# Attention scores of two heads from matmuls over the two halves of the array's rows

## The chip, the cores and the metric

The kernel runs on one core of one Trainium2 chip. The metric is the device time of one execution in microseconds (us). A core has TensorE (PE in the profile, its weight loads PEld), which multiplies a stationary operand, loaded beforehand, with a moving one and writes into PSUM; VectorE (DVE), ScalarE (ACT) and GpSimd (POOL), which work on SBUF and, the first two, on PSUM; and SyncE (SP), which issues the DMAs.

## The reference

Two decoder layers on a sequence of 512 tokens of width 1024, in float32. Layer 0 runs two groups of heads side by side, layer 1 one group of 16 heads; each is followed by a projection, a layer norm and a squared-ReLU MLP. What matters here are the scores, each a product of a query and a key of 64 numbers per head:

```python
# layer 0, A: 4 heads x 2 maps
s = jnp.einsum('bqhcd,bshcd->bhcqs', qb, kr)
p = jax.nn.softmax(jnp.where(mask, s, -jnp.inf), axis=-1)
pd = p[:, :, 0] - lam * p[:, :, 1]
...
# layer 0, B: 8 query heads on 2 k/v groups; compressed, selected and window branch
sc = jnp.einsum('bqghd,bngd->bghqn', qb, kc)
ss = jnp.where(valid_s, jnp.einsum('bqghd,bgqkld->bghqkl', qb, kg), -jnp.inf)
sw = jnp.einsum('bqghd,bsgd->bghqs', qb, kwb)
...
# layer 1, C: 16 heads with a cumulative forget bias
s = jnp.einsum('bqhd,bshd->bhqs', qb, kf) + cq[..., None] - c[:, :, None, :]
p = jax.nn.softmax(jnp.where(mask, s, -jnp.inf), axis=-1)
return jnp.einsum('bhqs,bshd->bqhd', p, vf)
```

With these sizes the selected branch covers all earlier tokens and the window all of the sequence, so both are causal softmaxes over 512 keys. That makes 8 + 16 + 16 = 40 causal softmaxes of one head each: 8 in A, 16 in B (8 heads, 2 branches), 16 in C.

## The kernel before

TensorE takes operands in fp32r, a float32 form of less precision. To keep float32 accuracy the kernel splits each operand into a high part (rounded to fp32r) and a low part (the rest) and adds three products: high x high, high x low, low x high. A head has only 64 rows of q and k, so the high and low part of one head are stacked on the 128 partitions. `stacks_q` (line 233) makes one tile with q's high part on one half and its low part on the other; `stacks_k` (line 250) makes two tiles, `ka` with k's high and low part and `kb` with the same two exchanged. In `softmax` (line 262) two matmuls over 128 rows, lines 270 and 271, then give all four products of a head (the low x low one comes for free). `split2` (line 243) makes each high and low part for one head of 64 partitions; lines 257 and 258 copy k's parts into the exchanged tile.

`softmax` goes over four tiles of 128 queries. Tile i has scores against (i+1) x 128 keys, so the moving operand is 128, 256, 384 and 512 columns wide. The scores fall into a PSUM bank of the tag "s", of which there are two. Line 274 (VectorE) adds the mask or the bias and takes a minimum, line 275 (ScalarE) makes the exponential and its sum. `scale_p` divides by the sums; `transpose_p` turns the probabilities by TensorE (line 288), through the tag "t", and splits them; `pv` (lines 303, 304) multiplies them with V.

Layer 0's attention runs the pieces of `EVEN_ORDER`: projections of q, k, v (`nat_chunk`, lines 180 to 182), compression, the branches, the heads of A (`diff_head`) and pairs of heads of B (`nsa_pair`). `nsa_pair` begins with the compressed branch: lines 810 and 811 multiply over 64 rows only. Layer 1's attention (`odd_attention`) goes over four groups of four heads; its projections of q and k are in `tr_block` (lines 193 to 195).

The order on each engine is not the order of the code: when the program is built, a scheduler places each instruction where it expects its inputs to be ready, so that TensorE's projections, transposes and products with V of one head stand between the scores of another. On the chip each engine takes its instructions in that built order.

Of the kernel before, what the change touches and what calls it, by code (L numbers as in the profile page):

```python
# [15 lines left out]
P = 128  # L16
SEQ = 512
NT = 4
# [13 lines left out]
QB = 6  # L32
KB = 6
# [27 lines left out]
def tile_trunk(ctx: ExitStack, tc: tile.TileContext, x, xt_in, ln_gain, ln_bias, w_up, w_down, w_ie, w_oe, lam_p, subln,  # L61
# [66 lines left out]
    lo_engine, rope_engine = [V], [V]  # L128

# [113 lines left out]
    def split2(src, hi, lo, scale):  # L243
        A.activation(hi, src, AF.Copy, scale=scale)
        if scale == 1.0:
            V.tensor_tensor(lo, src, hi.bitcast(F32), op=ALU.subtract)
        else:
            V.scalar_tensor_tensor(lo, src, scale, hi.bitcast(F32), op0=ALU.mult, op1=ALU.subtract)
# [12 lines left out]

    def softmax(ap, q, k, bias=None):

        p = new(ap, "p", [P, 1280], bufs=2)
        sm = new(ap, "sm", [P, 8], bufs=4)
        for i in range(NT):
            w = (i + 1) * P
            s = bank("s")
            qs = slice(i * P, (i + 1) * P)
            T.matmul(s[:, :w], q[:, qs], k[0][:, :w], start=True, stop=False)  # L270
            T.matmul(s[:, :w], q[:, qs], k[1][:, :w], start=False, stop=True)
            pv = p[:, OFF[i]:OFF[i] + w]
            add = mask[:, 512 - w:512] if bias is None else bias[:, OFF[i]:OFF[i] + w]
            V.tensor_tensor_reduce(pv, s[:, :w], add, 1.0, 3e38, ALU.add, ALU.min, sm[:, i:i + 1])  # L274
            A.activation(pv, pv, AF.Exp, bias=sm[:, i:i + 1], scale=-1.0, accum_out=sm[:, 4 + i:5 + i])  # L275
        return p, sm

# [857 lines left out]
```

## Time and profile before

| | us |
|---|---|
| median of 3 runs (lowest, highest) | 1274.55 (1274.54, 1275.23) |
| the profiled execution | 1273.6 |
| its span, first to last instruction | 1271.5 |
| TensorE busy | 1237.5 |
| VectorE busy | 878.2 |
| ScalarE busy | 647.3 |
| GpSimd busy | 301.2 |

The span is the time between the first and the last instruction that the profile shows; some 2 us of the execution lie around it. Busy time is the union of an engine's instructions. TensorE's matmuls are pipelined: the next one starts before the last one's end, so its durations add up to more than its busy time. The attention of layer 0 lies between about 60 and 300 us, that of layer 1 between about 680 and 890 us; the rest is projections and MLPs.

### The profile page before, as it was taken

What the parts mean: (1) busy time and instruction counts of PE and PEld (TensorE: products, weight loads), DVE (VectorE), ACT (ScalarE), POOL (GpSimd) and SP (SyncE); (2) the same over time, 40 slices, a digit from 0 to 9 for tenths busy, and PEclk for the clock granted to TensorE, in tenths of its full rate; (3) what the DMA queues carried; (4) which work ended last, traced back from release to release, by engine and by line L of the source; (5) the groups of instructions that cost most, each with busy time, mean ns of one, the idle gap of its engine ahead of it and who ended that gap; (6) DMA issues with size and microseconds to landing.
All of it is one profiled execution on the core that took longest, in us unless ns stands there. A gap on an engine that the chain in (4) does not pass through costs nothing.

```text
span 1271.5 us, 18398 instructions
## 1 busy us (share of the span) xinstructions
PE 1237.5 (97%) x7046; PEld 1079.2 (85%) x7046; DVE 878.2 (69%) x1602; ACT 647.3 (51%) x1185; POOL 301.2 (24%) x321
## 2 busy tenths in 40 slices
PE   7999998998999999999998999999999999999997
PEld 7999897898988888888887889889988888888886
DVE  5476768787859478495456788879767948669454
ACT  5266766764355454454423576767334445354530
POOL 1125565354200000000044354556510000000012
PEclk9999999999999999999999999999999999999999
DMA  7321121034414405234014322323630522505201
GB/s 274 114 87 54 34 67 35 5 129 138 167 61 132 133 25 175 67 96 146 17 50 150 101 84 92 92 88 129 231 112 23 182 84 68 164 34 159 73 17 50
DMA packets 46758, 125.15 MB, mean 98 GB/s; under 512 B 4672, under 2 KB 5184, under 8 KB 46672
## 3 DMA queue, kind: packets, MB, share of 16 engines
q1 hardware_dynamic: 46672, 123.99, 30.3%
q8 instruction: 55, 0.90, 0.3%
q14 instruction: 31, 0.25, 0.1%
HBM read 119.75 MB, written 4.23 MB: 98 GB/s over the span
## 4 chain that ended last, share of the span: by engine, by line
PE 86%; DVE 6%; DMA 3%; ACT 2%; issue 1%; POOL 1%; SPq 0%; DVEq 0%; ACTq 0%; POOLq 0%
PE g L193 11%; PE g L194 11%; PE g L195 11%; PE g L180 4%; PE g L181 4%; PE g L182 4%; PE s L478 3%; PE t L288 3%; PE s L479 3%; PE s L480 2%; DMA wraw<-w_up 2%; PE s L270 2%; PE o L480 2%; PE t L478 2%; PE o L478 2%; PE o L479 2%
## 5 line engine op out<-in xcount | busy, mean ns | idle before, releaser
L194 PE MATMUL g<-big,wlo 128*128 128x512 f32 x608 | 236.8, 391 | 0.0
L195 PE MATMUL g<-big,whi 128*128 128x512 f32 x608 | 236.6, 390 | 0.0
L193 PE MATMUL g<-big,whi 128*128 128x512 f32 x608 | 236.3, 390 | 0.0
L144 ACT ACTIVATE whi<-wraw 128x1024 fp32r<-128x1024 f32 (+3 forms) x120 | 125.3, 1045 | 112.5 <-DMA wraw<-w_up 37.1
L212 POOL TENSOR_TENSOR ve<-ve,nhalf 128x1 f32<-128x1 f32 x16 | 15.9, 991 | 647.0 <-DVE ve L211 647.0
L145 DVE TENSOR_TENSOR wlo<-wraw,whi 128x1024 fp32r<-128x1024 f32 (+2 forms) x69 | 84.3, 1228 | 96.5 <-ACT whi L144 96.4
L145 POOL TENSOR_TENSOR wlo<-wraw,whi 128x1024 fp32r<-128x1024 f32 (+2 forms) x51 | 123.4, 2425 | 94.6 <-ACT whi L144 82.3
L195 PEld LDWEIGHTS g<-big,whi 128*128 128x128 f32 x608 | 114.2, 188 | 23.6
L193 PEld LDWEIGHTS g<-big,whi 128*128 128x128 f32 x608 | 114.2, 188 | 23.2 <-issue 0.2
L194 PEld LDWEIGHTS g<-big,wlo 128*128 128x128 f32 x608 | 114.1, 188 | 23.1
L180 PE MATMUL g<-whi,big 128*128 128x256 f32 (+2 forms) x416 | 120.3, 289 | 0.6 <-DVE fz L946 0.4
L182 PE MATMUL g<-whi,big 128*128 128x256 f32 (+2 forms) x416 | 119.6, 287 | 0.0
L181 PE MATMUL g<-wlo,big 128*128 128x256 f32 (+2 forms) x416 | 119.1, 286 | 0.0
L414 DVE TENSOR_TENSOR wlo<-wdr,whi 128x1024 fp32r<-128x1024 f32 x72 | 87.4, 1218 | 44.4 <-ACT whi L413 44.4
L275 ACT ACTIVATE p<-p,sm 128x128 f32<-128x128 f32 (+3 forms) x160 | 89.2, 558 | 45.7 <-DVE sm L274 44.5
L395 ACT ACTIVATE big<-g 128x512 f32<-128x512 f32 x64 | 38.2, 597 | 134.4 <-PE g L195 134.4
L413 ACT ACTIVATE whi<-wdr 128x1024 fp32r<-128x1024 f32 x72 | 75.9, 1055 | 48.2 <-PE t L480 29.6
L321 POOL TENSOR_TENSOR p<-p,rs 128x128 f32<-128x128 f32 (+2 forms) x108 | 71.5, 688 | 93.2 <-DVE rs L970 40.4
L180 PEld LDWEIGHTS g<-whi,big 128*128 128x128 f32 x416 | 79.1, 190 | 2.2 <-ACT fv L114 0.6
L182 PEld LDWEIGHTS g<-whi,big 128*128 128x128 f32 x416 | 79.1, 190 | 0.7 <-issue 0.4
L181 PEld LDWEIGHTS g<-wlo,big 128*128 128x128 f32 x416 | 79.1, 190 | 0.6
L116 DVE TENSOR_TENSOR ptl<-t,pth 128x384 fp32r<-128x384 f32 (+1 forms) x108 | 63.1, 595 | 21.1 <-ACT pth L114 20.4
(313 smaller groups left out, 3093.0 us busy)
## 6 DMA issues: line engine op xcount, KB each, us to landing
wraw<-w_up SPq DMA_DIRECT2D x64, 512.0 KB, 3.7
wdr<-w_down SPq DMA_DIRECT2D x64, 512.0 KB, 4.7
wraw<-w_io SPq DMA_DIRECT2D x22, 512.0 KB, 3.3
wraw<-w_ie SPq DMA_DIRECT2D x18, 512.0 KB, 3.7
v<-w SPq DMA_DIRECT2D x8, 512.0 KB, 5.2
wraw<-w_oe SPq DMA_DIRECT2D x8, 512.0 KB, 3.6
cb<-c_dram SPq DMA_DIRECT2D x16, 256.0 KB, 3.2
wraw<-w_oo SPq DMA_DIRECT2D x8, 512.0 KB, 3.4
```

The source lines that it names most:

```text
L144: A.activation(hi[:, c], raw[:, c], AF.Copy)
L145: (eng or lo_engine[0]).tensor_tensor(lo[:, c], raw[:, c], hi[:, c].bitcast(F32), op=ALU.subtract)
L180: T.matmul(bv[:, tt], xh, h, start=first, stop=False)
L181: T.matmul(bv[:, tt], xh, l, start=False, stop=False)
L182: T.matmul(bv[:, tt], xl, h, start=False, stop=last)
L193: T.matmul(b[:, a:e], h[:, cs], xh, start=k == 0, stop=False)
L194: T.matmul(b[:, a:e], l[:, cs], xh, start=False, stop=False)
L195: T.matmul(b[:, a:e], h[:, cs], xl, start=False, stop=k == 7)
L275: A.activation(pv, pv, AF.Exp, bias=sm[:, i:i + 1], scale=-1.0, accum_out=sm[:, 4 + i:5 + i])
L413: A.activation(hi, r, AF.Copy)
L414: V.tensor_tensor(lo, r, hi.bitcast(F32), op=ALU.subtract)
L478: T.matmul(bv, hh, us[m][0][:, k], start=first, stop=False, skip_group_check=True)
```

## The change

The high and low parts are no longer stacked within a head. Two heads share a tile: the first head's 64 rows on partitions 0 to 63, the second's on 64 to 127, with one tile for the high parts and one for the low (`pair_q`, `pair_k`; `both_k` where two query heads share one key head, so that it stands on both halves). Each of the three products of a head is a matmul over 64 rows, the two heads' in turn, into a bank of each head. Per tile of queries the pair has six matmuls of 64 rows, where it had four of 128 rows. A token asks the scheduler to keep the six in this order; other matmuls may stand between them. `diff_head` takes its two maps as the pair, `nsa_pair` two query heads, `odd_attention` two heads. `pv` now makes the transposes of a group just ahead of its products, and p has three (layer 0) or four (layer 1) buffers for two. In the compressed branch one matmul of 64 columns serves two heads, three per pair and query tile.

```diff
+    bufs_ = dict(q=3, k=5, p=3)
...
-    def stacks_q(ap, b, scale):
-        r = []
-        for e in range(2):
-            q = new(ap, "q", [P, SEQ], F32R, bufs=QB)
-            own, oth = slice(64 * e, 64 * e + 64), slice(64 - 64 * e, 128 - 64 * e)
-            split2(b[own], q[own], q[oth], scale)
-            r.append(q)
-        return r
-    def stacks_k(ap, b, tag, bufs):
-        r = []
-        for e in range(2):
-            ka = new(ap, tag + "a", [P, SEQ], F32R, bufs=bufs)
-            kb = new(ap, tag + "b", [P, SEQ], F32R, bufs=bufs)
-            own, oth = slice(64 * e, 64 * e + 64), slice(64 - 64 * e, 128 - 64 * e)
-            split2(b[own], ka[own], ka[oth], 1.0)
-            A.activation(kb[oth], ka[own].bitcast(F32), AF.Copy)
-            V.tensor_copy(kb[own], ka[oth].bitcast(F32))
-            r.append((ka, kb))
-        return r
+    def pair_q(ap, b, scale):
+        q = [new(ap, f"q{c}", [P, SEQ], F32R, bufs=bufs_["q"]) for c in "hl"]
+        split(b, q[0], q[1], scale)
+        return q
+    def pair_k(ap, b):
+        k = [new(ap, f"k{c}", [P, SEQ], F32R, bufs=bufs_["k"]) for c in "hl"]
+        split(b, k[0], k[1])
+        return k
+    def both_k(ap, b, e):
+        k = [new(ap, f"k{c}", [P, SEQ], F32R, bufs=bufs_["k"]) for c in "hl"]
+        own = slice(64 * e, 64 * e + 64)
+        for r in (own, slice(64 - 64 * e, 128 - 64 * e)):
+            A.activation(k[0][r], b[own], AF.Copy)
+            V.tensor_tensor(k[1][r], b[own], k[0][own].bitcast(F32), op=ALU.subtract)
+        return k
+    def in_order(tok, ins):
+        tc.stamp_issue_order_token(ins.ins, tok)
     def softmax(ap, q, k, bias=None):
-        p = new(ap, "p", [P, 1280], bufs=2)
-        sm = new(ap, "sm", [P, 8], bufs=4)
+        p = [new(ap, "p", [P, 1280], bufs=bufs_["p"]) for _ in range(2)]
+        sm = [new(ap, "sm", [P, 8], bufs=4) for _ in range(2)]
         for i in range(NT):
             w = (i + 1) * P
-            s = bank("s")
+            s = [bank("s") for _ in range(2)]
             qs = slice(i * P, (i + 1) * P)
-            T.matmul(s[:, :w], q[:, qs], k[0][:, :w], start=True, stop=False)
-            T.matmul(s[:, :w], q[:, qs], k[1][:, :w], start=False, stop=True)
-            pv = p[:, OFF[i]:OFF[i] + w]
...
+            tok = nm("scores")
+            for n, (a, c) in enumerate(((0, 0), (1, 0), (0, 1))):
+                for e in range(2):
+                    rows = slice(64 * e, 64 * e + 64)
+                    in_order(tok, T.matmul(s[e][:, :w], q[a][rows, qs], k[c][rows, :w], start=n == 0, stop=n == 2))
+            for e in range(2):
+                pv = p[e][:, OFF[i]:OFF[i] + w]
+                add = mask[:, 512 - w:512] if bias is None else bias[e][:, OFF[i]:OFF[i] + w]
+                V.tensor_tensor_reduce(pv, s[e][:, :w], add, 1.0, 3e38, ALU.add, ALU.min, sm[e][:, i:i + 1])
+                A.activation(pv, pv, AF.Exp, bias=sm[e][:, i:i + 1], scale=-1.0, accum_out=sm[e][:, 4 + i:5 + i])
...
+    def pv(ap, o, p, v, start, stop):
         for grp in ((0,), (1,), (2, 3)):
...
+            pt = transpose_p(ap, p, grp)
             for j in grp:
...
         def nsa_cmp(g, qs):
             b = bank("s")
             for i in range(NT):
-                for h in range(4):
-                    o_ = b[:, i * 128 + h * 32:i * 128 + h * 32 + 32]
-                    for a in range(2):
-                        T.matmul(o_, qs[h][:, i * P:(i + 1) * P], kcs[:, a, g * 32:g * 32 + 32], start=a == 0, stop=a == 1)
+                for pr in range(2):
+                    o_ = b[:, i * 128 + pr * 64:i * 128 + pr * 64 + 64]
+                    for n, (a, c) in enumerate(((0, 0), (1, 0), (0, 1))):
+                        T.matmul(o_, qs[pr][a][:, i * P:(i + 1) * P], kcs[:, c, g].rearrange("p e n -> p (e n)"),
+                                 start=n == 0, stop=n == 2)
...
         def diff_head(kb, qk, v, h):
-            qs, kk = qk
-            p1, s1 = softmax(ap, qs[1], kk[1])
-            p0, s0 = softmax(ap, qs[0], kk[0])
+            (p0, p1), (s0, s1) = softmax(ap, *qk)
...
     def odd_attention(ap, mh, ml):
         wi = Weights(w_io)
+        bufs_.update(q=2, k=2, p=4)
...
-                    p, sm = softmax(ap, qs[e], kk[e], bias)
...
+                p, sm = softmax(ap, q, k, bias)
```

How the built order of TensorE moves, at two places. The first is the odd layer's first group, at the widest tile of a head. Before (`s` are score banks, `nka`, `nkb` the stacked tiles of k, `g` banks of a projection, `whi`, `wlo` its weights):

```order
L195 MATMUL g_1225_7224<-big_1106_6440,whi_1179_7042 128x512
L270 MATMUL s_1189_7067<-nka_1171_7022,q_1168_6991 128x384
L271 MATMUL s_1189_7067<-nkb_1172_7023,q_1168_6991 128x384
L270 MATMUL s_1190_7072<-nka_1171_7022,q_1168_6991 128x512
L271 MATMUL s_1190_7072<-nkb_1172_7023,q_1168_6991 128x512
L180 MATMUL g_1278_7421<-whi_1272_7410,big_1103_6437 128x256
```

And now, where `kh`, `kl` are the pair's high and low parts of k, `qh`, `ql` those of q, and the two numbers of `s` are the two heads' banks; score matmuls are line 269 now, and the lines of `nat_chunk` are 179 to 181:

```order
L179 MATMUL g_1323_7508<-whi_1319_7450,big_1145_6477 128x256
L269 MATMUL s_1236_7128<-kh_1211_7058,qh_1208_7029 128x512
L180 MATMUL g_1323_7508<-wlo_1320_7451,big_1145_6477 128x256
L181 MATMUL g_1323_7508<-whi_1319_7450,big_1146_6478 128x256
L179 MATMUL g_1323_7508<-whi_1319_7450,big_1145_6477 128x256
L180 MATMUL g_1323_7508<-wlo_1320_7451,big_1145_6477 128x256
L269 MATMUL s_1237_7129<-kh_1211_7058,qh_1208_7029 128x512
L269 MATMUL s_1236_7128<-kh_1211_7058,ql_1209_7030 128x512
L269 MATMUL s_1237_7129<-kh_1211_7058,ql_1209_7030 128x512
L269 MATMUL s_1236_7128<-kl_1212_7059,qh_1208_7029 128x512
L269 MATMUL s_1237_7129<-kl_1212_7059,qh_1208_7029 128x512
L181 MATMUL g_1323_7508<-whi_1319_7450,big_1146_6478 128x256
```

The head's scores stood together with the next tile's; now the first of the pair's six stands by itself, four projection matmuls follow, then the other five. The second place is the even layer, B's pair 01, the scores of the second branch. Before (`pth`, `ptl` are split transposes, `ident` belongs to a transpose):

```order
L288 MATMUL t_218_1440<-ident_2_69,p_211_1411 128x128 x2
L270 MATMUL s_232_1490<-nka_127_911,q_79_572 128x512
L271 MATMUL s_232_1490<-nkb_128_912,q_79_572 128x512
L304 MATMUL o_176_1278<-ptl_208_1394,v_109_753 128x256
L303 MATMUL o_176_1278<-pth_207_1393,v_109_753 128x128
L304 MATMUL o_176_1278<-ptl_208_1394,v_109_753 128x128
L288 MATMUL t_221_1449<-ident_2_69,p_211_1411 128x128 x3
```

And now, at the same scores (line 286 is a transpose now, lines 303 and 304 are still the products with V):

```order
L269 MATMUL s_223_1429<-kl_128_914,qh_78_573 128x384
L304 MATMUL o_175_1263<-ptl_205_1373,v_89_595 128x512
L286 MATMUL t_209_1388<-ident_2_69,p_177_1269 128x128 x3
L303 MATMUL o_175_1263<-pth_207_1382,v_89_595 128x384
L304 MATMUL o_175_1263<-ptl_208_1383,v_89_595 128x384
L269 MATMUL s_225_1440<-kh_127_913,qh_78_573 128x512
L303 MATMUL o_175_1263<-pth_210_1392,v_89_595 128x256
L269 MATMUL s_226_1441<-kh_127_913,qh_78_573 128x512
L269 MATMUL s_225_1440<-kh_127_913,ql_79_574 128x512
```

Score matmuls stood in twos among transposes and products with V; they stand in sixes, or as one and five, among the same. Over the whole program the matmuls over 64 rows (scores, and the two of the compressed branch) stand in 129 unbroken runs (68 in layer 0, 61 in layer 1; 45 of them a single matmul, 38 of five, 17 of six), where before only lines 810 and 811 are such, in 8 runs of two.

## Rows read from the trace of the kernel before

**Rows 1.** The page: busy time of each engine, and the chain of waits by engine.
```profile
PE 1237.5 (97%) x7046; PEld 1079.2 (85%) x7046; DVE 878.2 (69%) x1602; ACT 647.3 (51%) x1185; POOL 301.2 (24%) x321
...
PE 86%; DVE 6%; DMA 3%; ACT 2%; issue 1%; POOL 1%; SPq 0%; DVEq 0%; ACTq 0%; POOLq 0%
```

**Rows 2.** Two stretches: start:end, length, then busy us of each engine (instructions), clock, DMA.
```profile
128.00:256.00 128.00, 120.19 (x871) 108.91 (x871) 96.96 (x277) 92.22 (x243) 68.80 (x114) 0.99 0.12 40
700.00:890.00 190.00, 189.56 (x1179) 167.88 (x1178) 155.41 (x355) 127.13 (x278) 96.74 (x78) 0.99 0.30 98
```

**Rows 3.** Groups by line and shape: count | busy us, mean ns | idle before.
```profile
L270 PE MATMUL s<-nka,q 128*128 128x512 f32 x40 | 16.7, 418 | 0.0
...
L271 PE MATMUL s<-nkb,q 128*128 128x128 f32 x40 | 11.0, 275 | 0.0
...
L258 DVE CAST nkb<-nka 64x512 fp32r<-64x512 f32 x28 | 15.6, 556 | 0.9
...
L246 DVE TENSOR_TENSOR nka<-g,nka 64x512 fp32r<-64x512 f32 x22 | 15.2, 689 | 1.6 <-ACT nka L244 1.0
```

**Rows 4.** Timeline of TensorE, odd layer: start us, duration us, line, tiles, shapes.
```profile
715.03 0.34 PE L270 MATMUL s<-nka,q 128*128 128x384 f32 x1
715.20 0.34 PE L271 MATMUL s<-nkb,q 128*128 128x384 f32 x1
715.38 0.39 PE L270 MATMUL s<-nka,q 128*128 128x512 f32 x1
715.61 0.40 PE L271 MATMUL s<-nkb,q 128*128 128x512 f32 x1
715.84 0.28 PE L180 MATMUL g<-whi,big 128*128 128x256 f32 x1
715.96 0.28 PE L181 MATMUL g<-wlo,big 128*128 128x256 f32 x1
...
718.48 0.22 PE L270 MATMUL s<-nka,q 128*128 128x128 f32 x1
718.53 0.28 PE L271 MATMUL s<-nkb,q 128*128 128x128 f32 x1
718.65 0.33 PE L181 MATMUL g<-wlo,big 128*128 128x256 f32 x1
718.82 0.28 PE L182 MATMUL g<-whi,big 128*128 128x256 f32 x1
```

**Rows 5.** Timeline of TensorE around lines 810 and 811, even layer.
```profile
97.85 0.28 PE L182 MATMUL g<-whi,big 128*128 128x256 f32 x1
98.06 0.49 PE L810 MATMUL o<-pch,vcb 64*128 64x512 f32 x1
98.39 0.39 PE L811 MATMUL o<-pcl,vcb 64*128 64x512 f32 x1
98.72 0.50 PE L270 MATMUL s<-nka,q 128*128 128x512 f32 x1
99.05 0.39 PE L271 MATMUL s<-nkb,q 128*128 128x512 f32 x1
```

**Rows 6.** The weight loads (PEld) of the same stretch.
```profile
97.73 0.19 PEld L182 LDWEIGHTS g<-whi,big 128*128 128x128 f32 x1
98.06 0.18 PEld L810 LDWEIGHTS o<-pch,vcb 64*128 64x128 f32 x1
98.16 0.19 PEld L811 LDWEIGHTS o<-pcl,vcb 64*128 64x128 f32 x1
98.71 0.19 PEld L270 LDWEIGHTS s<-nka,q 128*128 128x128 f32 x1 [0.36 <-issue]
98.82 0.19 PEld L271 LDWEIGHTS s<-nkb,q 128*128 128x128 f32 x1
```

**Rows 7.** Groups by line and shape: lines 810 and 811.
```profile
L810 PE MATMUL o<-pch,vcb 64*128 64x512 f32 x8 | 4.0, 494 | 1.4 <-DVE y L310 1.4
L811 PE MATMUL o<-pcl,vcb 64*128 64x512 f32 x8 | 3.1, 392 | 0.0
```

More of the change, by code (lines that the diff above doesn't have):

```diff
@@ L31 @@
 TB = 2
-QB = 6
-KB = 6
 EVEN_ORDER = "W C Q0 B0 B1 c0 D1 V01 P01 P00 D0 Q1 H0 c1 H1 P10 D3 P11 D2 V23 H3 H2".split()
@@ L276, in softmax, with transpose_p @@
         return p, sm
-    def transpose_p(ap, p):
+    def transpose_p(ap, p, grp):
         r = []
+        b = bank("t")
+        c = 0
+        at = []
+        for j in grp:
+            at.append(c)
+            for i in range(j, NT):
+                T.transpose(b[:, c:c + P], p[:, OFF[i] + j * P:OFF[i] + (j + 1) * P], ident)
+                c += P
+        hi = new(ap, "pth", [P, SEQ], F32R, bufs=4)
+        lo = new(ap, "ptl", [P, SEQ], F32R, bufs=4)
+        split(b[:, :c], hi[:, :c], lo[:, :c])
+        for a, j in zip(at, grp):
+            w = (NT - j) * P
+            r.append((hi[:, a:a + w], lo[:, a:a + w]))
+        return r
@@ L292, in transpose_p @@
-            split(b[:, :c], hi[:, :c], lo[:, :c])
-            for a, j in zip(at, grp):
-                w = (NT - j) * P
-                r.append((hi[:, a:a + w], lo[:, a:a + w]))
-        return r
-    def pv(o, pt, v, start, stop):
-        for j in range(NT):
-            h, l = pt[j]
-            os_ = o[:, j * P:SEQ]
-            T.matmul(os_, v(j), h, start=start and j == 0, stop=False)
-            T.matmul(os_, v(j), l, start=False, stop=stop and j == NT - 1)
+                h, l = pt[j - grp[0]]
@@ L306, in fold @@
+                os_ = o[:, j * P:SEQ]
+                T.matmul(os_, v(j), h, start=start and j == 0, stop=False)
+                T.matmul(os_, v(j), l, start=False, stop=stop and j == NT - 1)
     def fold(ap, o, y, e):
@@ L746, in branch @@
             gemm(evac)
-            ks.append(stacks_k(ap, transpose_nat(nats, 0, "o" if br == 0 else "s"), "nk", KB))
+            b = transpose_nat(nats, 0, "o" if br == 0 else "s")
+            ks.append([both_k(ap, b, g) for g in range(2)])
             vs.append(v)
@@ L766, in nsa_q @@
             gemm(evac)
-            qs = []
-            for pr in range(2):
-                qs += stacks_q(ap, transpose_nat(nats, 128 * pr, tag), 1.0)
-            return qs
+            return [pair_q(ap, transpose_nat(nats, 128 * pr, tag), 1.0) for pr in range(2)]
         def nsa_cmp(g, qs):
@@ L803, in nsa_pair @@
         def nsa_pair(g, pr, qs, pc):
[L804 removed]
+            y = new(ap, "nat", [P, SEQ], bufs=NB)
+            o = [bank("o") for _ in range(2)]
             for e in range(2):
[L806 to L807 removed]
                 rows = slice(64 * pr, 64 * pr + 64)
                 vc = vcb[rows, g, e].rearrange("p a c -> p (a c)")
[L810 to L820 removed]
+                T.matmul(o[e], vc, pc[0][rows], start=True, stop=False)
+                T.matmul(o[e], vc, pc[1][rows], start=False, stop=False)
+            for br in range(2):
+                p, sm = softmax(ap, qs[pr], ks[br][g])
+                for e in range(2):
+                    r = new(ap, "rs", [P, 4], bufs=4)
+                    V.reciprocal(r, sm[e][:, 4:8])
+                    V.tensor_tensor(r, r, gv[:, :, 4 * g + 2 * pr + e, 1 + br], op=ALU.mult)
+                    scale_p(p[e], r)
+                    pv(ap, o[e], p[e], lambda j: vs[br][:, j, g].rearrange("p a c -> p (a c)"), False, br == 1)
+            for e in range(2):
+                fold(ap, o[e], y, e)
             kb = 4 + 2 * g + pr
@@ L978, in forget @@
     def forget(ap, fz):
-        tri = new(ap, "y", [P, SEQ])
+        tri = new(ap, "ft", [P, SEQ], bufs=TB)
         nc.sync.dma_start(out=tri, in_=consts[:, C_TRI:C_TRI + 512])
```

77 lines of the change are left out of this document (25 added, 52 removed).

## The prediction

> **What bounds the kernel now.** I read the page's busy times and its chain of waits first, then busy time by stretch, then the timeline of TensorE's matmuls and weight loads. TensorE is busy 97% of the span and 86% of the chain that ended last is its own [rows 1]. So the question is how much of TensorE's time the change takes or gives, and whether some stretch has room to hide it. In the odd layer there is none: of 190 us TensorE is busy 189.56 [rows 2]. In the even layer there is a little: between 128 and 256 it is busy 120.19 of 128 us, so it idles 7.8 [rows 2].
>
> "Busy" says little here, since a matmul's duration (0.28 us for 256 columns) overlaps the next one's. What counts is the step from one start to the next, which I call a slot. 384 columns: 715.03 to 715.38 for two, 0.175 us each. 512 columns: 715.38 to 715.84 for two, 0.23. 256 columns: 715.84 to 715.96, 0.12 [rows 4]. 128 columns: from 718.48 to 718.82 there are two of 128 and one of 256, so about 0.11 each [rows 4]. 128 columns are no cheaper than 256: every matmul here brings new weights, and weight loads start 0.10 to 0.12 us apart at best [rows 6]. So a slot is the time to stream the columns (0.23 us for 512, half for 256), but not under 0.11 us.
>
> **Part 1: the score matmuls themselves.** There are 40 of each width for each of the two lines, 320 in all [rows 3]: 40 heads' softmaxes, four widths, two matmuls. In slots: 0.11 + 0.12 + 0.175 + 0.23 = 0.635 us, times 80, is 51 us. After it there are 20 pairs of heads with six matmuls per width, 480 in all, each over 64 rows. The trace has no two matmuls on the two halves of the array, so I bound what they cost:
> - Upper bound C, nothing overlaps: 120 x 0.635 = 76 us, 25 us more than now.
> - Lower bound A, the halves load and stream fully side by side: where the six stand together, three slots. The built order, however, often parts them: 45 times a single score matmul stands alone ahead of a run of five, and a run of five needs three slots itself. Going through the built order and taking one slot per two neighbours of a run gives 45 us, 6 us less than now.
> - Between them B, streams overlap but weight loads go one after another, at the 0.11 us of [rows 6]: a run of n costs n x 0.11 us or its paired streams, whichever is more. Over the built order this is 57 us, 6 us more.
> I take B. The row nearest to it is the pair of 64-row loads at 98.06 and 98.16 [rows 6]: half the rows, yet the load takes as long as one of 128 rows (98.71 to 98.82), and two successive ones are never closer. The ends, -6 and +25 us, go into the range.
>
> **Part 2: going into the 64-row form and out again.** This is the largest term. The kernel already has 64-row matmuls: lines 810 and 811, eight of each [rows 7], always as a pair among 128-row work. At 97.85 a 128-row matmul of 256 columns starts; the next would follow at 97.97, and with two of 512 columns between them the one after at 98.43 and the one behind it at 98.66. In the trace that last one (line 271) starts at 99.05 [rows 5]: 0.39 to 0.40 us late. The loads show where it goes [rows 6]. Between 128-row matmuls the next load starts while the last one streams, every 0.12 us. The load of line 810 starts at 98.06, 0.33 us after the load before it, about 0.1 us after the last stream has ended; that of line 270 starts at 98.71, 0.32 us after line 811's start, again 0.1 us after its stream. Within the pair no such gap: 98.06 to 98.16. So at each change of form the array runs empty (0.1 us) and then the first load has no stream to hide under (another 0.1): 0.2 us in and 0.2 us out. The profile puts the gap before line 270's load down to "issue": that load waited for nothing [rows 6]. And the eight pairs are alike: the mean of line 810 is 0.10 us over that of line 811, which is the unhidden load [rows 7]. The Trainium skill (TensorEngine Tiling (Array Packing), Key Properties) says the same in one line: changing the tiling mode, as opposed to the tile, drains TensorE.
>
> How often does the changed kernel pay this? The order of instructions decides it. The scheduler fills between score tiles with projection matmuls, transposes and products with V, all of 128 rows, as the second place in the part on the change shows. In the built order the 64-row matmuls (scores and the two of lines 810/811) form 129 separate runs, where they formed 8: 68 in the even layer, 61 in the odd one. 121 more runs x 0.40 us = 48 us. A run of a single 128-wide matmul pays some hundredths less.
>
> **Part 3: the rest.** The pair's q and k are split over all 128 partitions in one go, and the copies into the second stack fall away: 51 rows fewer on VectorE and as many on ScalarE in the built order, at 0.56 to 0.69 us each on VectorE [rows 3]. I count them at nothing where TensorE never waits (the odd layer), and in the even layer together with the next item. The products with V now follow each group of transposes, p has more buffers, and the compressed scores have 48 matmuls for 64: under 2 us, in the same waits.
>
> **Part 4: what is absorbed.** Added TensorE time hides only where TensorE waits: the 7.8 us between 128 and 256 [rows 2]. The two-at-a-time scores also hold both score banks until two maskings (lines 274) are done, which can make new waits where little filler is left. I take -5 us, between -8 (all of it) and +10.
>
> **Sum.** B: +6 + 48 - 5 = +49 us on the profiled execution's 1273.6 us (span 1271.5) is 1322.6; the median of the runs lies 1 us above that execution, so 1324.
>
> **The rivals.**
> - A, halves load and stream side by side: -6 + 48 - 5 = +37, 1312 us. For it: the two halves have rows of their own. Against it: no two loads in the trace are closer than 0.1 us at 128 columns.
> - C, the halves take turns: +25 + 48 - 5 = +68, 1343 us. For it: every matmul in the trace takes a slot of its own, and none streams beside another. Against it: nothing in the trace says that two halves must take turns, since none ever tried.
> - D, changing the half drains as changing the form does: some 350 changes of half within the runs x 0.2 us = 70 us on top of C, 1413 us. Lines 810 and 811 stay on one half, so the trace can't exclude it.
> - E, on the other side: faster. The array takes 64-row matmuls in among 128-row ones without running empty, and what [rows 5, 6] show comes of those two lines alone, say of what they wait for. Then part 2 is nothing, A's 6 us are gained and 0 to 2 us of waits go with VectorE's work: 1267 us. It decides where a change of form costs under 0.05 us. Against it: the gap also stands in front of line 270's load, which waits for nothing, and on both sides of the pair.
> The Trainium skill (TensorE: Matmul & The Clock Gate, Measured speedup vs the span model) has row packing at 3.07 times for four tiles of 32 rows and 512 columns, and TensorEngine Tiling (Theoretical Speedup) up to two times for 64 rows. By two times alone, with no drain and no split runs, the scores would fall from 51 to 38 us, which is E with about 1261; no run here shows any packing, and the gaps of [rows 6] speak against it.
> - The change might not do what it says: matmuls told to stand together may not (45 lone ones show that already); this is in the numbers above.
>
> **How the numbers follow.** B 0.34, A 0.26, C 0.24, D 0.05, E 0.07; 0.04 is for a change within the resolution, where a change of form costs only about 0.1 us. Forecast 1324 us. A to C with their absorbed waits reach from about 1303 (A with all waits used and lone runs cheaper) to 1348 (C with none used); 0.84 of the chance lies there, so this is the range. A measurement of this kernel tells apart about 0.2% (2.5 us): faster 0.07, same 0.04, slower 0.89.
>
> **What would show it.** Right: in the changed kernel's timeline a gap of about 0.3 us between the start of loads at each change between 128 and 64 rows, and a stretch of the odd layer, where TensorE has no waits, longer by some 61 x 0.4 = 24 us plus its share of the matmuls. B against A and C: six 512-wide score matmuls in a row take about 0.69 us in all by A and by B, 1.4 by C; six 128-wide ones 0.33 by A, 0.66 by B and C. Wrong: loads of 64 and 128 rows that follow each other at 0.12 us; a granted clock at its lower level where the array runs empty more often (it is 0.99 in both stretches of [rows 2]); or new waits of TensorE for line 274.

## The result and the profile after

| | before | after |
|---|---|---|
| median, us (lowest, highest; 4 runs each) | 1274.55 (1273.25, 1275.23) | 1380.91 (1380.00, 1385.82) |
| ratio after/before, 95% interval | | 1.084 (1.082 to 1.086) |
| profiled execution: span, us | 1271.5 | 1379.0 |
| mean granted clock of TensorE (1 is full speed) | 0.994 | 0.959 |

The change costs 106 us. The sign was forecast; the size was not: 1324 was forecast, and 1381 lies above the range (1303 to 1348).

The page of after, in the lines that answer to [rows 1], with TensorE's clock (40 slices of 34.5 us, in tenths of full speed):

```profile
PE 1321.2 (96%) x7190; PEld 1105.5 (80%) x7190; DVE 844.6 (61%) x1552; ACT 617.5 (45%) x1136; POOL 301.4 (22%) x322
...
PEclk9999795689999999999999999999999999999999
...
PE 88%; DVE 4%; ACT 3%; DMA 2%; POOL 1%; issue 1%; SPq 0%; DVEq 0%; ACTq 0%; POOLq 0%
```

TensorE is about as busy as before by its share (96% for 97%), VectorE and ScalarE have 34 and 30 us less to do, and the span is 107 us longer. The new thing is the PEclk row: slices 5 to 9 (138 to 310 us, layer 0's attention) show 0.7, 0.9, 0.5, 0.6 and 0.8 (each digit rounded down) where all others show 0.9.

The two stretches that answer to [rows 2] (start:end, length, busy us of PE, PEld, DVE, ACT, POOL, clock, DMA):

```profile
128.00:256.00 128.00, 106.92 (x557) 82.27 (x554) 67.67 (x186) 55.39 (x155) 41.80 (x70) 0.73 0.06 19
790.00:980.00 190.00, 188.70 (x1110) 151.54 (x1108) 115.30 (x295) 96.66 (x223) 86.92 (x69) 1.00 0.27 92
```

In layer 0 TensorE was busy 120.19 of 128 us at a clock of 0.99; now it is 106.92 at 0.73, so it waits 21 us for 8, and what it does takes longer. In layer 1 nothing of the kind: busy 188.70 of 190, clock 1.00. So the time is cut by stage, from the first matmul of a stage to the last of its output projection. "Slots" is what the matmuls of the stage would take one after another at the full clock, by the median step from one start to the next in the trace of before (0.11 us up to 128 columns, 0.12 for 256, 0.175 for 384, 0.227 for 512, and 0.125 and 0.13 for the few of 272 and 280); "waits" is TensorE's idle time before instructions; a change of form is a step from a 128-row matmul to a 64-row one or back:

| | layer 0 attention, us | slots | waits | changes of form | layer 1 attention, us | slots | waits | changes |
|---|---|---|---|---|---|---|---|---|
| before | 321.5 | 293 | 12.3 | 18 | 253.3 | 242 | 4.4 | 0 |
| after | 401.9 | 306 | 30.9 | 140 | 280.5 | 252 | 9.6 | 122 |

The MLPs are the same in both (342.2 and 339.7 us before, 342.5 and 339.3 after). Layer 1 costs 27.2 us more, layer 0 80.4.

The waits that are new in layer 0 of after (95 to 350 us) are TensorE's for other engines. The largest is the one that the prediction named, of the scores for the masking (line 274 then, 273 now), with its total, number and longest:

```profile
PE s L269 <- DVE sm L273: 6.7, 15, 0.8
```

In before it is 0.2 us. Then come the transposes, which wait 6.5 us for GpSimd's scaling of the probabilities (line 321) and 6.4 for the subtraction of two maps (line 859; 2.5 in before).

### The profile page after: what moved, and what is told of

It reads as the page before. It is cut to its first block, busy times and chain, and to the rows that moved or that the text cites. A ratio compares the mean times of both kernels' runs of the same rounds, so it can differ in the third digit from the quotient of the medians.

```text
span 1379.0 us, 18627 instructions
## 1 busy us (share of the span) xinstructions
PE 1321.2 (96%) x7190; PEld 1105.5 (80%) x7190; DVE 844.6 (61%) x1552; ACT 617.5 (45%) x1136; POOL 301.4 (22%) x322
## 4 chain that ended last, share of the span: by engine, by line
PE 88%; DVE 4%; ACT 3%; DMA 2%; POOL 1%; issue 1%; SPq 0%; DVEq 0%; ACTq 0%; POOLq 0%
PE g L193 11%; PE g L192 11%; PE g L194 10%; PE s L269 5%; PE g L179 4%; PE g L180 4%; PE g L181 4%; PE t L286 3%; PE s L478 2%; PE s L479 2%; PE s L480 2%; PE o L304 2%; PE o L303 2%; PE o L478 2%; PE o L480 2%; PE o L479 2%
## 5 line engine op out<-in xcount | busy, mean ns | idle before, releaser
L180 PE MATMUL g<-wlo,big 128*128 128x256 f32 (+2 forms) x416 | 121.4, 292 | 0.0
L286 PE MATMUL t<-ident,p 128*128 128x128 f32 x360 | 74.5, 326 | 14.0 <-POOL p L321 7.3
L112 ACT ACTIVATE pth<-t 128x384 fp32r<-128x384 f32 (+1 forms) x108 | 54.5, 524 | 74.2 <-PE t L286 73.0
L180 PEld LDWEIGHTS g<-wlo,big 128*128 128x128 f32 x416 | 80.5, 194 | 3.7 <-issue 3.1
```

The lines of the kernel that those rows point to most:

```text
L180: T.matmul(bv[:, tt], xh, l, start=False, stop=False)
L286: T.transpose(b[:, c:c + P], p[:, OFF[i] + j * P:OFF[i] + (j + 1) * P], ident)
```

## The experiments

Two theories stood at first. A detour is the way into the 64-row form and out again. **F**: it costs more than 0.40 us in layer 0. **S**: the matmuls cost what the prediction says, and layer 0's extra comes from something else in the change. The change alters two more things there: `y`, in which a pair of heads is collected, no longer has a buffer of its own but takes one of the three of the ring `nat`, which the projections' results need too; and two heads are held in step, so that a pair takes two of the three buffers of `p` (a head took one of two). The expectations count the theories otherwise: their theory 1 puts all on the changes of form, theory 2 on the buffer of `y`, theory 3 on two heads in step. Each of e1 to e7 and e9 to e11 ran once; runs of one kernel lie within 7 us of one another here.

### The form and the two halves

**e4_l1_only**: the change in layer 1 alone; layer 0 as before.

```diff
-                    p, sm = softmax(ap, qs[e], kk[e], bias)
+                p, sm = softmax_pair(ap, q, k, bias)
```

> The change in layer 1 alone, layer 0 as before. All theories that price layer 1 by the change of form: 61 runs x 0.4, less 3 us of side by side matmuls, so the 27 us that layer 1 grew by in the changed kernel: 1300 us. If the two layers hang together (the clock, a transfer that shifts): off that by more than 5 us.

Measured: 1298.47 us, layer 1 at 278.7, layer 0 at 321.5 as before. Layer 1 is 25.4 us longer than before: 122 changes of form at 0.2 us are 24.4, the scores take 1.7 less (below), and TensorE waits 2.6 more, 25.3 in all. The part with no room to hide anything costs what was added up for it.

**e2_half_single**: heads one at a time as before, but three matmuls over 64 rows for each score tile, in 167 runs.

```diff
-            T.matmul(s[:, :w], q[:, qs], k[0][:, :w], start=True, stop=False)
-            T.matmul(s[:, :w], q[:, qs], k[1][:, :w], start=False, stop=True)
+            rows = slice(64 * e, 64 * e + 64)
+            for n, (a, c) in enumerate(((0, 0), (1, 0), (0, 1))):
+                T.matmul(s[:, :w], q[a][rows, qs], k[c][rows, :w], start=n == 0, stop=n == 2)
```

> The structure of the kernel before (one head at a time, y with its own buffer) with scores of three 64-row matmuls. 167 runs of 64-row matmuls, 159 more than before, and no two halves side by side. Theory 1: 159 x 0.4 + 25 us for the serial matmuls = +89, less some waits: 1350 to 1364. Theory 2: the same, with projections spread evenly and the clock near full in layer 0. If the clock falls because of the form changes themselves: 1380 or more, with a granted clock under 0.9 in layer 0.

Measured: 1359.25 us; layer 0 372.4, layer 1 289.3. It has more detours than after (208 changes of form in layer 0) and no pairing, yet layer 0 is 30 us shorter than in after: F falls. Its timeline of TensorE (start, duration, line, shapes) shows the price with nothing else in it:

```profile
936.45 0.33 PE L295 MATMUL o<-ptl,fv 128*128 128x384 f32 x1
936.71 0.50 PE L262 MATMUL s<-kh,qh 64*128 64x512 f32 x1
937.04 0.39 PE L262 MATMUL s<-kh,ql 64*128 64x512 f32 x1
937.28 0.39 PE L262 MATMUL s<-kl,qh 64*128 64x512 f32 x1
937.60 0.50 PE L192 MATMUL g<-big,whi 128*128 128x512 f32 x1
937.94 0.40 PE L193 MATMUL g<-big,wlo 128*128 128x512 f32 x1
```

Four steps are longer than their slots, by 0.09 to 0.11 us each: line 295 to the first score (0.26 for 0.17), the first score (0.33 for 0.23), the last one (0.32 for 0.23) and line 192 (0.34 for 0.23). That is 0.2 us in and 0.2 us out.

Now six matmuls, three on each half, in after (x2 stands for two that start together):

```profile
98.11 0.39 PE L269 MATMUL s<-kh,qh 64*128 64x256 f32 x2
98.33 0.28 PE L269 MATMUL s<-kh,ql 64*128 64x256 f32 x2
98.45 0.29 PE L269 MATMUL s<-kl,qh 64*128 64x256 f32 x2
98.67 0.39 PE L179 MATMUL g<-whi,big 128*128 128x256 f32 x1
```

And the loads at both ends of that run:

```profile
98.11 0.19 PEld L269 LDWEIGHTS s<-kh,qh 64*128 64x128 f32 x2 [0.17 <-DVE sm L273]
...
98.67 0.19 PEld L179 LDWEIGHTS g<-whi,big 128*128 128x128 f32 x1
```

The two halves load and stream together, their starts mostly 3 to 4 ns apart; a run of six costs what three cost alone. The medians of the runs at the full clock, from the first start to that of the next 128-row matmul, say it for every width (of the sixes, those whose first two start together; at 512 columns that is one in after and one in e4):

| columns | lone matmul (after) | three on one half (e2) | five (after) | six, the halves in turn (after, e4) |
|---|---|---|---|---|
| 128 | 0.25 us | 0.48 | 0.48 | – |
| 256 | 0.31 | 0.55 | 0.54 | 0.55 |
| 384 | 0.37 | 0.72 | 0.72 | 0.72 |
| 512 | 0.43 | 0.89 | 0.89 | 0.89 |

The Trainium skill (TensorEngine Tiling (Array Packing), Key Properties) has tiles load and multiply in parallel; the trace agrees. It is rival A, not B. The table also prices the order: the five cost as much as six, so the lone matmul ahead of them costs its 0.25 to 0.43 us on top, and the outer halves of one more way in and out. And side by side is had only when both heads' banks are free: two other sixes of 512 columns in after take 1.20 and 1.37 us, since the second head's first matmul starts 0.30 and 0.48 us behind the first's; in the longer one its weight load waits for the masking (line 273).

**e9_l1_serial**: e4 with the loops exchanged, so that one head's three matmuls come before the other's.

```diff
-            for n, (a, c) in enumerate(((0, 0), (1, 0), (0, 1))):
-                for e in range(2):
+            for e in range(2):
+                for n, (a, c) in enumerate(((0, 0), (1, 0), (0, 1))):
```

> e4_l1_only (the change in the odd layer alone), with one exchange of loops: in each width the three matmuls of one head come first and then the three of the other, where e4 alternates the two heads, that is the two halves of the array. Same matmuls, same buffers; in the built order 64 runs of 64-row matmuls for e4's 69, which by 0.40 us a run is 2 us less. If the two halves load and stream side by side (rival A of the prediction), alternating is what gains, and the odd layer takes 8 to 12 us more than e4's 278.7 less these 2: 285 to 289, 1305 to 1309 in all. If only streams overlap (B): about 3 us more, 1301. If the halves take turns in any case (C): no loss, 1296 to 1299.

Measured: 1304.80 us; layer 1 282.9, 4.2 more than e4, under the 6 to 10 expected. Layer 0, which is that of before in both, came out 2.6 us longer in e9, so a difference of 4.2 between two single runs says little by itself. The runs say more: time inside 64-row runs in layer 1, less waits and less 0.205 us for each run (the part of a detour that falls inside it), is 18.5 us in e4, 24.7 in e9, 29.1 in e2 (30.2 as slots one after another; the stacked scores of before are 20.2). So e9 lost 6.2 us and gained 2 by five runs fewer. But the reason was not the one expected. Where three and three stand together they run side by side all the same, though in the built order the second head's first matmul comes after the first head's third:

```profile
908.07 0.50 PE L315 MATMUL s<-kh,qh 64*128 64x512 f32 x2
908.40 0.40 PE L315 MATMUL s<-kh,ql 64*128 64x512 f32 x2
908.63 0.40 PE L315 MATMUL s<-kl,qh 64*128 64x512 f32 x2
908.97 0.39 PE L409 MATMUL g<-whi,big 128*128 128x256 f32 x1
```

0.90 us for six, their starts 10 ns apart. So the sentence ahead of the prediction that each engine takes its instructions in the built order does not hold for the starts of matmuls on two halves. What e9 lost, it lost because the scheduler put 38 of its runs as threes, each head's alone between 128-row matmuls, with nothing on the other half.

### Where layer 0's time goes

**e1_stack_pair**: the changed kernel's pairs, `p` and `y`, but scores stacked over 128 rows, two matmuls a head, so that no score changes the form. It also has the compressed scores and the q and k of before, and three buffers of `pth` and `ptl` for four.

```diff
-            for n, (a, c) in enumerate(((0, 0), (1, 0), (0, 1))):
-                for e in range(2):
-                    rows = slice(64 * e, 64 * e + 64)
-                    in_order(tok, T.matmul(s[e][:, :w], q[a][rows, qs], k[c][rows, :w], start=n == 0, stop=n == 2))
+            for e in range(2):
+                T.matmul(s[e][:, :w], q[e][:, qs], k[e][0][:, :w], start=True, stop=False)
+                T.matmul(s[e][:, :w], q[e][:, qs], k[e][1][:, :w], start=False, stop=True)
```

> The pair structure of the changed kernel (two heads at a time, y in the ring of the tag nat, p with 3 and 4 buffers) with the stacked 128-row scores of the kernel before. Theory 1 (the price is the change of form, 0.4 us a run, in both layers): nothing of it is left, about 1275 us. Theory 2 (in layer 0 the tile y takes one of the three nat buffers that the projections need; projections are pushed together, TensorE waits between and its clock falls): layer 1 back to 253 us, layer 0 still long, about 1310 to 1335. Theory 3 (two heads in lockstep hold both score banks and two of three p buffers) gives the same as theory 2 here.

Measured: 1328.59 us: layer 0 371.2, that is 49.7 more than before without one 64-row score; layer 1 only 4.8 more. S stands. Two theories on what in the pair's structure costs it: **P**, the shared buffer of `y`; **L**, two heads in step.

**e5_before_ynat** changes one line of the kernel before:

```diff
-            y = new(ap, "y", [P, SEQ], bufs=1)
+            y = new(ap, "nat", [P, SEQ], bufs=NB)
```

> The kernel before, with one change: the even layer's buffer y (which collects the two heads of a pair for the output projection) is taken from the three buffers that the projections' results use, as the changed kernel does, in place of a buffer of its own. Heads still one at a time, scores still stacked over 128 rows, the number of 64-row matmuls unchanged. Theory P (the changed kernel's extra loss in the even layer comes from that shared buffer: projections can no longer be issued between the softmaxes, so TensorE is left without filler and its clock falls): the even layer takes 30 to 50 us more, 1300 to 1325 in all, with a granted clock visibly under 1 between 100 and 350 us. Theory L (it comes from two heads being held in step, with both score banks taken until both maskings are done): within 5 us of the kernel before, 1275 to 1280.

**e6_stack_pair_yown** is e1 with that line put back; a temporary tile of the compressed branch again takes `y`'s buffer, as in before, and one ring of small tiles (`rs`) has three buffers for four.

> Two heads in step, as in the changed kernel, but the scores stay stacked over 128 rows (no additional 64-row matmul), and y has a buffer of its own again. It is e1_stack_pair with y's buffer put back. Theory P: nearly all of e1's 54 us go, 1275 to 1290. Theory L: it stays near e1, 1318 to 1330. Both at work: between, about 1300.

Measured: e5 1310.45 (layer 0 +33.1), e6 1299.23 (layer 0 +17.8). Both are at work, and 33.1 + 17.8 = 50.9 is about e1's 49.7; some of the 17.8 may be the smaller rings'. How P works is seen in busy time of one of the projection's three lines (L180: the first of the three in before and e5, the second in after and e11) between 132 and 168 us (busy us of PE and PEld with their instructions, clock, DMA). Before:

```profile
132.00:168.00 36.00, 12.25 (x43) 8.29 (x44) 1.00 0.14 41
```

After:

```profile
132.00:168.00 36.00, 0.00 (x0) 0.00 (x0) 0.69 0.01 1
```

e5, and behind it e11, which comes below:

```profile
132.00:168.00 36.00, 0.97 (x2) 0.78 (x3) 0.81 0.04 14
```

```profile
132.00:168.00 36.00, 9.11 (x32) 6.08 (x32) 0.91 0.09 30
```

43 matmuls of that line stood there before, as filler between the softmaxes; in after none (nor any of its other two lines), and with one line changed in e5 two. The projections come later, in a lump, and TensorE is left with work that waits for other engines.

**e3_y_own** (after, with `y` a buffer of its own and `ptl` three), **e10_p4** (after, with four buffers of `p` in layer 0 and three of `pth` and `ptl`) and **e11_p4_yown** (both, with four pairs of k in place of five) do the same on the changed kernel.

```diff
-    bufs_ = dict(q=3, k=5, p=3)
+    bufs_ = dict(q=3, k=4, p=4)
...
-            y = new(ap, "nat", [P, SEQ], bufs=NB)
+            y = new(ap, "y", [P, SEQ], bufs=1)
```

> The changed kernel with a buffer of its own for y in layer 0 (and one buffer of ptl fewer to make room). 141 runs of 64-row matmuls. Theory 2: projections spread again, the clock in layer 0 near full, layer 0 at 322 + 27 to 35 = 349 to 357 us, in all 1325 to 1335. Theory 3: within 10 us of the changed kernel, 1370 to 1385. Theory 1 alone: 1385, since there are more runs.

> The changed kernel with four buffers for the probabilities p in the even layer in place of three (two pairs of heads in place of one and a half), and three for the transposed probabilities in place of four to make room. If holding two heads in step costs time since the next pair's p is missing, the even layer comes down by 10 to 20 us, 1361 to 1371. If it comes from the score banks, which both wait for both maskings, or only from y's shared buffer: within 4 us of the changed kernel, 1377 to 1385.

> e3_y_own (the changed kernel with a buffer of its own for y) with four buffers for p in the even layer and four in place of five for the pairs of k to make room. If the missing p is what the lockstep costs: 10 to 20 us under e3's 1357.6, 1338 to 1348, which leaves the detours into the 64-row form (some 55 us) and the longer slots less the gain of side by side as all that the change costs. If the score banks are: within 4 us of e3, 1354 to 1361.

| layer 0 attention, us (whole kernel) | `p` three | `p` four |
|---|---|---|
| `y` in the ring | 401.9 (after, 1380.9) | 376.9 (e10, 1355.0) |
| `y` its own | 378.9 (e3, 1357.6) | 348.1 (e11, 1328.1) |

Each gives 23 to 31 us with or without the other, both together 53.8 of the 80.4. That L works by `p` and not by the score banks is seen in VectorE's waits between 95 and 350 us (total, times, longest), in before, in after and then in e3:

```profile
DVE p L274 <- PE t L288: 2.5, 6, 0.8
```

```profile
DVE p L273 <- PE t L286: 11.4, 6, 2.9
```

```profile
DVE p L273 <- PE t L286: 17.6, 8, 3.2
```

The masking of the next pair waits until the transposes have emptied a `p`. In e6, without a 64-row score, this wait is 10.0 us; in e10 and e11, with four buffers of `p`, it stands in neither list.

What is left in e11 over before in layer 0, 26.6 us, is about what the forms cost: 138 changes x 0.2 = 27.6, less about 3 for scores side by side (estimate: layer 1's 20.2 - 18.5 us for 16 heads, times 24/16), and 1.4 us more waits. That leaves nothing for the clock, which by the estimate of the next part would take another 9 us there.

### The clock

After by stretches of 2 and 4 us, where a pair's transposes wait for the subtraction of two maps (`p`, line 859):

```profile
208.00:212.00 4.00, 3.90 (x33) 3.59 (x31) 3.67 (x7) 1.86 (x2) 3.46 (x4) 1.00 0.00 0
212.00:216.00 4.00, 0.69 (x2) 0.29 (x2) 4.00 (x2) 0.00 (x0) 3.81 (x2) 0.69 0.39 127
216.00:218.00 2.00, 1.46 (x5) 1.06 (x6) 0.59 (x2) 0.98 (x2) 0.00 (x0) 0.50 0.57 168
218.00:222.00 4.00, 4.00 (x20) 3.77 (x19) 1.77 (x4) 1.29 (x5) 0.00 (x0) 0.50 0.13 51
```

The timeline of the same place:

```profile
213.66 0.69 PE L286 MATMUL t<-ident,p 128*128 128x128 f32 x2 [1.76 <-DVE p L859]
216.28 1.12 PE L286 MATMUL t<-ident,p 128*128 128x128 f32 x4 [1.92 <-DVE p L859]
```

TensorE is busy 3.90 of 4 us at 1.00, then 0.69 of 4, and the granted clock goes to 0.50, the lower of its two levels (1.2 GHz); it is still there in the next 4 us, in which TensorE never waits. What that costs: the same six 512-wide scores at 0.50 (249 to 251 us) and at 1.00 (layer 1), to the start of the next matmul:

```profile
249.86 0.79 PE L269 MATMUL s<-kh,qh 64*128 64x512 f32 x2
250.45 0.63 PE L269 MATMUL s<-kh,ql 64*128 64x512 f32 x2
250.88 0.49 PE L269 MATMUL s<-kl,qh 64*128 64x512 f32 x2
251.31 0.44 PE L887 MATMUL o<-ident,ft 128*128 128x128 f32 x2
```

```profile
964.23 0.50 PE L269 MATMUL s<-kh,qh 64*128 64x512 f32 x2
964.57 0.40 PE L269 MATMUL s<-kh,ql 64*128 64x512 f32 x2
964.81 0.39 PE L269 MATMUL s<-kl,qh 64*128 64x512 f32 x2
965.12 0.39 PE L335 MATMUL g<-whi,big 128*128 128x256 f32 x1
```

1.45 us against 0.89. By stretches of 40 us, 120 to 280, before:

```profile
120.00:160.00 40.00, 38.13 (x279) 34.63 (x278) 29.28 (x84) 29.81 (x74) 22.27 (x38) 1.00 0.08 27
160.00:200.00 40.00, 40.00 (x331) 39.57 (x330) 26.95 (x78) 26.33 (x68) 25.20 (x47) 1.00 0.17 54
200.00:240.00 40.00, 34.43 (x210) 27.96 (x209) 35.00 (x102) 30.64 (x88) 19.94 (x30) 0.96 0.09 27
240.00:280.00 40.00, 39.63 (x312) 38.17 (x313) 30.28 (x81) 25.30 (x61) 18.13 (x16) 1.00 0.29 99
```

And after:

```profile
120.00:160.00 40.00, 37.31 (x184) 25.85 (x182) 25.02 (x75) 23.53 (x64) 13.63 (x15) 0.79 0.08 27
160.00:200.00 40.00, 34.07 (x206) 29.25 (x206) 9.66 (x26) 13.45 (x31) 17.81 (x41) 0.83 0.08 27
200.00:240.00 40.00, 29.51 (x157) 22.75 (x156) 26.25 (x65) 16.24 (x46) 11.77 (x11) 0.67 0.08 27
240.00:280.00 40.00, 34.72 (x145) 25.01 (x145) 23.68 (x69) 19.41 (x58) 9.18 (x14) 0.65 0.00 1
```

Busy time x (1 - clock), summed over the 40-us stretches from 120 to 360, is 43.6 us in after and 2.8 in before: an estimate of 41 us for the clock, beside 18.6 us more waits. It counts all busy time at 0.50 as doubled, but the six scores above took 1.6 times as long.

Waits are not the whole of it. In e2, where TensorE waits less in layer 0 than in before (7.4 us for 12.3), the clock fell at 224 us, behind a wait, and stayed at 0.50 for 34 us in which TensorE was never idle but for 0.05 us:

```profile
224.00:258.00 34.00, 33.95 (x107) 24.75 (x108) 15.67 (x55) 14.82 (x49) 7.04 (x11) 0.50 0.03 12
```

Low stretches of 20 us and more stand in after, e2, e3 and e10, which all have 64-row scores in layer 0, and none over 14 us in before, e1, e5, e6 and e12, which have none there; but e7 and e11 have such scores and no stretch over 14 us either. Whether the 64-row work itself helps to hold the clock down was not tested.

**e7_warm** tried to part the two: three idle matmuls of 128 rows and 512 columns ahead of each head's first transposes in layer 0, their results overwritten.

```diff
+        if grp[0] == 0 and bufs_["p"] == 3:
+            for _ in range(3):
+                T.matmul(b, xTh[0][:, 0, 0:P], xTh[0][:, 0, :], start=True, stop=True)
```

> The changed kernel with idle work added in the even layer: three matmuls of 128 rows and 512 columns into the bank of the transposed probabilities, ahead of the first transposes of each of the heads there, overwritten by these and used by nothing. At the 0.23 us of a slot that is some 14 to 23 us of work more. Theory K (in the even layer the time is lost since the granted clock falls when TensorE waits, so all its work there takes longer): the added work fills waits, the granted clock between 100 and 340 us rises from the 0.65 to 0.86 of the changed kernel to 0.85 or more, and the time falls or stays, 1340 to 1381. Rival (the clock only follows the waits and costs nothing itself): the clock stays, and the time grows by part or all of the added work, 1385 to 1405.

Measured: 1393.42 us; layer 0 413.1, 11.2 more than after, for some 13.6 us of added work (60 matmuls at 0.227). The clock in the same four stretches rose from 0.79, 0.83, 0.67, 0.65 to 0.83, 0.87, 0.76, 0.76, short of what the theory needed; TensorE's waits rose by 4.7 us. The time grew as the rival has it, but the clock rose in part, which the rival has not. By the estimate above the higher clock gave back 8.9 us; 13.6 + 4.7 - 8.9 is 9.4, near the 11.2, which speaks for the estimate. But the clock was not brought back, so the run doesn't show what a full clock would be worth in this order, and that share is not settled by an experiment.

### Two trials on the kernel before

**e8_before_cmp128** makes its eight 64-row pairs over 128 rows, with zeros in the other rows (and has three buffers of `ptl` for four).

```diff
-                vc = vcb[rows, g, e].rearrange("p a c -> p (a c)")
-                T.matmul(o, vc, pc[0][rows], start=True, stop=False)
-                T.matmul(o, vc, pc[1][rows], start=False, stop=False)
+                vc = vcb[:, g, h].rearrange("p a c -> p (a c)")
+                T.matmul(o, vc, pc[0], start=True, stop=False)
+                T.matmul(o, vc, pc[1], start=False, stop=False)
```

> The kernel before, with its only 64-row matmuls (the products with the compressed values, lines 810 and 811, eight pairs) made over 128 rows: the values stand in a matrix of their own for each head, with zeros in the other rows, and everything else is unchanged apart from one buffer fewer for the low parts of the transposed probabilities, to make room. If a detour into the 64-row form and back costs 0.40 us of TensorE's time, 8 pairs less give 3.2 us: 1271.4, ratio 0.9975. If the gaps around those pairs were waits of another kind, no change: 1274 to 1275.

Measured: ratio 0.9998 (0.9987 to 1.0009), no difference, where 0.9975 was expected. The rows that answer to [rows 5]:

```profile
98.49 0.28 PE L182 MATMUL g<-whi,big 128*128 128x256 f32 x1
98.61 0.40 PE L809 MATMUL o<-pch,vcb 128*128 128x512 f32 x1
98.84 0.40 PE L810 MATMUL o<-pcl,vcb 128*128 128x512 f32 x1
99.08 0.39 PE L270 MATMUL s<-nka,q 128*128 128x512 f32 x1
99.31 0.40 PE L271 MATMUL s<-nkb,q 128*128 128x512 f32 x1
```

From line 182 to line 271 it is 0.82 us, where it was 1.20: the detour's 0.38 us are gone, and so at five more of the eight places (0.34 to 0.39 us each, by the two traces laid side by side); at two, TensorE waits for `y` there anyway, and nothing is gained. But later waits took most of it back: by the same comparison all or part of the gain of three places is gone again at the next waits for VectorE or ScalarE. Layer 0 takes 320.9 us for 321.5.

**e12_before_p3** gives the kernel before three buffers of `p`, paid for with one each of `pth`, `ptl` and q.

```diff
-        p = new(ap, "p", [P, 1280], bufs=2)
+        p = new(ap, "p", [P, 1280], bufs=3)
...
-            hi = new(ap, "pth", [P, SEQ], F32R, bufs=4)
-            lo = new(ap, "ptl", [P, SEQ], F32R, bufs=4)
+            hi = new(ap, "pth", [P, SEQ], F32R, bufs=3)
+            lo = new(ap, "ptl", [P, SEQ], F32R, bufs=3)
```

> The kernel before (one head at a time) with three buffers for the probabilities p in place of two, in both layers; to make room the transposed probabilities get three in place of four and the stacked q five in place of six. If too few buffers of p cost the kernel before as they cost the changed one, its TensorE waits in the even layer (12.3 us in attention and output projection) and the 2.5 us in which VectorE's maskings wait for the transposes shrink: 1266 to 1272, ratio 0.994 to 0.998. If two are enough for one head at a time, no difference, or up to 4 us more from the smaller rings: ratio 0.999 to 1.003.

Measured: 1285.21 us, ratio 1.0086 (1.0068 to 1.0104), slower than either theory said: 5.1 us in layer 0, 5.0 in layer 1, and 7.2 us of waits of the scores for line 274 in layer 0, 0.2 in before (all waits there: 15.4 for 12.3). Whether the smaller rings or another built order does it was not parted. No version here beats the kernel before.

## Why the prediction was wrong

**Part 2, the changes of form, held.** 0.2 us in and 0.2 us out, at every width, wherever the clock is 1.00. Its 48 us are in the result.

**Part 1 took the wrong case, and it mattered little.** B (+6) was taken from the 0.1 us between two successive loads of lines 810 and 811 [rows 6]. But those two stand on the same half; no row of before had loads on two halves, and the nearest row was of another kind. A holds: in layer 1 the scores take 18.5 us where they took 20.2, so about -4 over both layers (estimate, by 40/16 heads).

**Layer 1 came out near the forecast, in part by luck.** The prediction's 24 us and its share of B (+2.4, 16 of 40 heads) make 27; measured 27.2. But the scores took 1.7 less, not 2.4 more, and 5.2 us of new waits, which it put at nothing, took their place: 24.4 - 1.7 + 5.2 = 27.9. Most of these stand at the stage's ends (2.4 us more at line 1011, 2.1 at line 357). e4, with 2.6 us of new waits, adds up too.

**The step that failed is part 4, what is absorbed, with the sentence of part 3 that lets the products with V, the buffers of `p` and the rest go "in the same waits" for under 2 us.** It gave layer 0 between -8 and +10 us. The runs show some 59 us in its place (80.4 less 24.4 for forms, plus 3 for scores): 18.6 us waits and, by the estimate above, 41 us lower clock. The same accounting closes to within 2 or 3 us on e3, e5, e6 and e10; on e1 it is 7 us short, on e11 8 us too high, and on e2 12 us too high (38 for forms, 13 for the added matmuls, 4.8 less waits, 16.5 for the clock: 63 for 50.9). So the share of the clock is good to some 10 us; it is an accounting, while the causes, `y` in the projections' ring and three buffers of `p` for pairs, are shown by e5, e6 and the table of four. The prediction did name "new waits where little filler is left" and a fallen clock as what would make it wrong, but priced neither. Two things were there to be read. `y` going into the ring `nat` is a line of the whole diff (the cut one ahead of the prediction leaves it out), and none of its text follows that line to the projections that want the same buffers. And [rows 2] show 7.8 us of waits at a clock of 0.99: they say how much filler was just enough, not how much was to spare.

**Corrected sum:** 48 - 4 + 5 + 59 = 108; the spans differ by 107.5 us. The last term is what is left over in layer 0, so the sum closes there by construction; only layer 1 and e4 test the working. Against the forecast of +49, part 4 was 64 us too low, layer 1's waits add 5, and part 1 was 10 too high.

**The other rivals.** C (the halves take turns) and D (a change of half drains) are out by the starts 3 to 4 ns apart, and by six in the time of three. E, faster, needed a change of form under 0.05 us; it is 0.2. In a run, six side by side save at best one slot of 0.23 us against the four stacked matmuls, and the way in and out costs 0.40: split runs or not, with a run for each score tile this change can't pay here; with the buffers of e11 it still takes 1328.1 us.

## What to carry to other kernels

Work on two row halves does run side by side, but the way into the 64-row form and back cost 0.4 us here; it pays only where a run is long enough to save more than that. A buffer moved into a shared ring, or a ring that holds fewer units of work than before, is a change of its own: ask which other work wants the same buffers, since that work may be the filler that keeps TensorE from waiting. Where TensorE begins to wait, price what follows at the lower clock too, and not only the waits.

## What the runs showed of the hardware

- Two 64-row matmuls on different halves mostly start 3 to 4 ns apart, loads and streams both, and a run of six takes the time of three (0.89 us at 512 columns). The Trainium skill (TensorE: Matmul & The Clock Gate, Measured speedup vs the span model) gives about 4 ns per tile; the trace agrees.
- The order within an unbroken run of six hardly matters: with three of one head and then three of the other, the second head's first starts 10 ns after the first head's first, ahead of two matmuls that stand before it in the built order (0.90 us for six). What does matter is that the second head's bank is free: where it was not, six took up to 1.37 us.
- The way from 128-row to 64-row matmuls costs 0.2 us, and the way back another 0.2 (e2: four steps 0.09 to 0.11 us longer than their slots).
- A detour of 0.4 us removed is worth 0.4 us only where no wait follows: eight removed in layer 0 of the kernel before gave no difference that could be measured.
- In layer 0 of after the granted clock fell to 0.50 where TensorE was busy 0.69 of 4 us, and it was 0.50 still over 4 us in which TensorE was busy throughout. In e2 it stayed at 0.50 for 34 us in which TensorE was busy 33.95.
